# RWKV's small transposes made whole-array ones, token statistics taken from a second, row-wise load of x, and the readers of five broadcasts tied to a weight chunk

## The chip, the cores and the metric

The kernel runs on one core of one Trainium2 chip. The time is the device time of one execution in microseconds, and the time of a kernel is the median of its runs. A core has five engines, each with an instruction stream of its own that runs in program order: TensorE (PE, with its weight loads PEld), VectorE (DVE), ScalarE (ACT), GpSimd (POOL) and SyncE (SP), which here issues the weight transfers.

## The reference, cut to what matters

One block of a model over 256 tokens of width 2048 in float32: a projection of the normed input feeds four branches (an RG-LRU, a forgetting attention "fox", an SSD, an RWKV-7 recurrence), their outputs are gated and merged, and a feed-forward and a gated embedding follow.

```python
xn = rmsnorm(h, mix_norm)                       # mean of squares over 2048 features
proj = xn @ w_in                                # 2048 x 15,000 or so columns
y_a = rg_lru_branch(a_x, a_g, ...)
y_b = forgetting_attention_branch(b_q, b_k, ...)   # q and k normed per head
y_c = mamba2_branch(c_z, c_xbc, c_dt, ...)         # output normed per group
y_d = rwkv7_branch(d_u, ...)
merged = sum(sigmoid(g_j) * (y_j @ w_branch[j]))
h = h + merged @ w_out
h = h + (gelu(conv(hn @ w_up)[gate]) * conv(hn @ w_up)[val]) @ w_down
h = h + sigmoid(rmsnorm(h) @ w_ple_gate) * (p @ w_ple)
```

Inside `rwkv7_branch` the key is normed per head, and the state of each of the eight heads (64 x 64) is advanced token by token; the output is normed per head (mean, variance, `ln_w`, `ln_b`).

## The kernel before, in words

All activations lie feature-major: 128 features on the partitions, 256 tokens along a row. The weights, some 310 MB, are streamed once from HBM in chunks of 512 KB (tile wr, four buffers, line 205, all on SyncE's queue). A matmul in full float32 precision is made of two halves: `split` (lines 208 to 214) has ScalarE round a chunk to its high half wh (the cast, line 212) and VectorE subtract to get the low half wl (line 213), three buffers each. `product` (line 239) then issues a 512-column matmul for wh (the activation's high and low half side by side) and a 256-column one for wl. `gemm_fm` (lines 256 to 302) runs over the chunks of one unit of weights and over its blocks of 128 output features, and keeps the sums in PSUM (tile pg; the branches use pb). So each chunk needs, in this order, its transfer, ScalarE's cast, VectorE's subtraction, and TensorE.

The branches are Python generators (lru, ssd, fox, rwkv). After every block of a product `gemm_fm` calls `hook[0]`, which is `pump` (line 1050): it advances the generator that is first in line by a step, if the credit it keeps allows one. A step's `yield n` says how much credit it costs. `lane` sets one of three priorities (products, branches, TensorE), and a scheduler orders each engine's instructions by these priorities and the dependences, with no knowledge of how long a transfer takes. An engine that reaches an instruction whose input is not there waits, and all that stands behind it on that engine waits with it.

The start: x is loaded feature-major (xT) by `load_x` (line 374) in eight tiles xraw of two feature blocks each. ScalarE squares each tile (line 389), GpSimd sums the squares (line 391), and `token_rstd` (line 401) sums over the partitions with a matmul against ones and takes the reciprocal square root; the result is R (a value per token, on all partitions), and rcol, the same with tokens on partitions. The first unit of weights, w_ax, is multiplied as x arrives; `evac_raw` (line 412) copies its sums out and multiplies by R. `load_after` (line 422) has GpSimd write one column of a tile from another tile, so that the load that ScalarE's queue then issues can't start before that other tile is there. The constants cbr come this way; cbr holds the identity among others.

Five times a branch computes a small row per head, which must then be had on all partitions. GpSimd writes it to DRAM (`bcast_rows`, line 459) and reads it back spread over the partitions (`bcast_full`, `bcast_half`, `head_bcast`, lines 465, 471, 762). The five are ssd_ac (read into tiles d and e; the d tile E is exponentiated on ScalarE, line 693), ssd_rn (line 737), fox_rn (read with the tile gain, line 574), rw_kn (line 831) and rw_gn (line 1009). For rw_gn the source row is finished by a Newton step of two instructions on 8 partitions (`sb<-sb 8x256`), and the first reader on VectorE is `sb<-sb,prm,d`.

The recurrence of RWKV (lines 928 to 986) goes in four blocks of 64 tokens. For each block it loads a tile jc (name e in the profile), transposes three of its parts per head, value and two keys (the last block only the value), with `heads` (line 937): 64 x 64 at a time, the lower head by a matmul with a piece of the identity and the upper one by a transpose (lines 946 to 949), eight per part. A float32 matmul leaves two records in the profile, a transpose one, so a part is 12 records. `kept` (line 953) copies the 128 x 256 result to SBUF.

Of the kernel before, what the change touches and what calls it, by code (L numbers as in the profile page):

```python
# [7 lines left out]
F32 = mybir.dt.float32  # L8
# [3 lines left out]
ALU = mybir.AluOpType  # L12
# [73 lines left out]
def body(tc, T, out, dbg=None):  # L86
# [18 lines left out]
    def add(o, a, b):  # L105
        tt(o, a, b, ALU.add)
# [100 lines left out]

    def split(wr, kn, cols):

        wh = wp.tile([P, kn, cols], F32R, name="wh", tag="wh", bufs=3)  # L210
        wl = wp.tile([P, kn, cols], F32R, name="wl", tag="wl", bufs=3)
        A.copy(wh, wr)  # L212
        V.tensor_tensor(wl, wr, wh.bitcast(F32), op=ALU.subtract)  # L213
        return [(wh[:, i], wl[:, i]) for i in range(kn)]
# [159 lines left out]
    def load_x(k0, kn):  # L374

        if k0 == KD:
            add(xraw[0][:, :S], xraw[0][:, :S], xraw[0][:, S:])
            token_rstd(xraw[0][:, :S], R, rcol)
            return
        xd = xraw[k0 // 2][:, (k0 % 2) * S:(k0 % 2) * S + kn * S]  # L380
        dma_w.dma_start(xd.rearrange("p (k t) -> p k t", k=kn),
                            T["xT"][k0 * P:k0 * P + kn * P].rearrange("(k p) t -> p k t", p=P))
        for k in range(k0, k0 + kn):
            xr = xraw[k // 2][:, (k % 2) * S:(k % 2) * S + S]
            xs.append(split_x(xr, mixc[:, k:k + 1]))
        k = k0 + kn - 1
        if k % 2:
            s = xraw[k // 2]
            act(s, s, AF.Square)
            if k > 1:  # L390
                G.tensor_tensor(xraw[0], xraw[0], s, op=ALU.add)
# [9 lines left out]
    def token_rstd(acc, Rt, col):  # L401
        pt = bank()
        mm2(pt[:, :S], ones_r, acc)
        rstd_of(Rt, pt[:, :S], float(D), EPS, slot(), slot())
        if col is not None:
            pt = bank()
            for t in range(2):
                mm(pt[:, t:t + 1], acc[:, t * P:t * P + P], ones[:, 0:1])
            rstd_of(col, pt[:, :2], float(D), EPS, slot()[:, :2], slot()[:, :2])
    raw = {"ax": []}  # L410

    def evac_raw(lst):
        def f(m, pt):
            s = bslot()
            joined(s, pt)
            mul(s, s, R)
            lst.append(s)
        return f

    gemm_fm(T["w_ax"], xs, evac_raw(raw["ax"]), load_x)  # L420
# [7 lines left out]
    def eslot(shape):  # L428
        return bc_.tile(shape, F32, name="e", tag="e", bufs=3)

# [107 lines left out]
    def fox():  # L538
# [12 lines left out]
        gain = bc_.tile([P, 2], F32, name="gain")  # L551
        ts(gain[:, 0:1], pc("fox_q_gain", 0), 128.0 ** -0.5)
        ts(gain[:, 1:2], pc("fox_k_gain", 0), 1.0)
# [16 lines left out]
        yield  # L570
        qn = []
# [51 lines left out]
    def ssd():  # L623
# [69 lines left out]
        act(E, E, AF.Exp)  # L693
# [40 lines left out]
        yield 6  # L734
        res = []
        for j in range(4):
            stt(yt[j], yt[j], pc("ssd_norm", j), rbc[:, j // 2], ALU.mult, ALU.mult)
# [35 lines left out]
    def rwkv():  # L773
# [26 lines left out]
        yield 6  # L800
        pend = bc_.tile([P, 4, 4], F32, name="pend")
# [6 lines left out]
        for j in range(4):  # L808
# [22 lines left out]
            stt(kk, k_[j], pc("rwkv_kk", j), nbc[j], ALU.mult, ALU.mult)  # L831
# [99 lines left out]
        for c in range(4):  # L931
# [5 lines left out]
            def heads(terms, pt=None):  # L937


                pt = bank() if pt is None else pt  # L940
                for j in range(4):
                    for i, (l, r) in enumerate(terms):
                        for h in (1, 0):
                            hs = H2[h]
                            o = pt[hs, j * 64:j * 64 + 64]
                            if h == 0 and r is ident:
                                transpose(o, l[hs, j], ident[hs, hs])
                                continue
                            mm(o, l[hs, j], r[hs, j] if r is not ident else ident[hs, hs],
                               start=i == 0, stop=i == len(terms) - 1)  # L950
                return pt[:, :S]
# [8 lines left out]
            vc = kept(heads([(jc[:, :, 3], ident)]))  # L960
            yield
            if c < 3:
                btk = kept(heads([(jc[:, :, 1], ident)]))
                yield
                ktk = kept(heads([(jc[:, :, 2], ident)]))
                yield
# [115 lines left out]

    proj("ag", 0, 2)
# [114 lines left out]
    token_rstd(acc1[0], R2, None)  # L1198
# [47 lines left out]
    token_rstd(acc2[0], R3, None)  # L1246
# [31 lines left out]
def layout(inputs):  # L1278
# [11 lines left out]
    for n in ("w_out", "w_up", "w_down", "w_ple_gate"):  # L1290
        r[n] = tiles(f[n][0], S, 4)
    r["xT"] = np.ascontiguousarray(f["x"][0].T)
# [39 lines left out]
```

## Time and profile before

| what | value |
|---|---|
| runs | 1750.37, 1761.89, 1765.18 us (median 1761.89) |
| profiled execution | 1751.44 us |
| its span, first to last instruction | 1749.6 us |
| mean granted clock of TensorE | 0.995 |
| TensorE busy | 1730.1 us (99%), 11621 matmuls |
| VectorE, ScalarE, GpSimd busy | 1237.7 (71%), 942.9 (54%), 102.8 us (6%) |
| HBM read, written | 324.85 MB, 9.48 MB; 191 GB/s over the span |

A row of a timeline gives the start in us from the span's beginning, the time until the last of the xN instructions ended, the engine, the line, the operation, `output<-inputs` by the program's names, the shape, and in brackets how long the engine was idle before it and what ended that. In a row of windows each engine has its busy time and, in parentheses, its number of instructions; the last three columns are the granted clock of TensorE, the busy share of the DMA engines and GB/s.

### The profile page before, as it was taken

Reading aid. Unit: us, or ns where it says so; the run is one execution under the profiler, and the core shown is the slowest. Engines: PE = TensorE matmul, PEld = TensorE weight load, DVE = VectorE, ACT = ScalarE, POOL = GpSimd, SP = SyncE. Lnnn points to the kernel's source line nnn. Section 1 sums busy time; section 2 is a strip of 40 time slices with the busy share of each in tenths; the row PEclk is TensorE's granted clock in tenths of the full one; section 3 lists DMA queues with packets and bytes.
Section 4 is the critical chain, followed back from the end, with each engine's and each line's share of the span. In section 5 each row is a group of like instructions: output and inputs, shape, how many; then the busy total and the mean of one; then the engine's idle time right before and its main releaser. Section 6 shows DMA issues by size and latency. Waiting matters only on the chain.

```text
span 1749.6 us, 29736 instructions
## 1 busy us (share of the span) xinstructions
PE 1730.1 (99%) x11621; PEld 1567.8 (90%) x11621; DVE 1237.7 (71%) x1998; ACT 942.9 (54%) x1422; POOL 102.8 (6%) x160
## 2 busy tenths in 40 slices
PE   8999999999999999999999999999999999999998
PEld 6888888999999989999888888888888888888887
DVE  7788767677789732668678777777777765555666
ACT  6586445556644433545556555555555544444554
POOL 4000000002320100000110000000000000000000
PEclk9999999999999999999999999999999999999999
DMA  7555556556675743565776666656666666656573
GB/s 265 172 178 188 180 174 214 188 183 207 205 214 175 248 137 118 175 198 185 237 227 188 189 190 192 191 186 190 192 189 197 214 208 189 193 190 191 171 227 133
DMA packets 98844, 336.27 MB, mean 192 GB/s; under 512 B 12330, under 2 KB 16592, under 8 KB 98704
## 3 DMA queue, kind: packets, MB, share of 16 engines
q1 hardware_dynamic: 90528, 310.94, 56.3%
q0 software_dynamic: 7456, 21.81, 4.3%
q8 instruction: 91, 1.49, 0.4%
q10 hardware_dynamic: 720, 1.63, 0.3%
q14 instruction: 49, 0.40, 0.1%
HBM read 324.85 MB, written 9.48 MB: 191 GB/s over the span
## 4 chain that ended last, share of the span: by engine, by line
PE 82%; DVE 1%; DMA 0%; issue 0%; ACT 0%; POOLq 0%
PE pg L132 78%; PE pb L135 4%; PE pb L132 1%; DMA e<-fox_rn 0%; DVE wl L213 0%; DVE sb L100 0%; DVE sb L120 0%; DVE s L100 0%; DMA fox_rn<-sb 0%; ACT s L253 0%; POOLq L466 0%
## 5 line engine op out<-in xcount | busy, mean ns | idle before, releaser
L132 PE MATMUL pg<-x,wh 128*128 128x512 f32 (+1 forms) x4384 | 1172.3, 340 | 3.4 <-DVE sb L100 2.7
L213 DVE TENSOR_TENSOR wl<-wr,wh 128x1024 fp32r<-128x1024 f32 (+1 forms) x592 | 716.9, 1212 | 419.6 <-ACT wh L212 412.6
L212 ACT CAST wh<-wr 128x1024 fp32r<-128x1024 f32 (+1 forms) x592 | 615.4, 1041 | 645.7 <-PE pg L132 503.3
L132 PE MATMUL pg<-x,wl 128*128 128x256 f32 (+1 forms) x3344 | 919.7, 283 | 8.8 <-DVE wl L213 8.8
L132 PEld LDWEIGHTS pg<-x,wh 128*128 128x128 f32 x4384 | 748.0, 188 | 89.8 <-issue 4.0
L132 PEld LDWEIGHTS pg<-x,wl 128*128 128x128 f32 (+1 forms) x3344 | 630.4, 189 | 23.7 <-DVE wl L213 11.6
L132 PE MATMUL pg<-f,wh 128*128 128x512 f32 x704 | 243.2, 391 | 0.0
L132 PE MATMUL pg<-f,wl 128*128 128x256 f32 x704 | 195.8, 282 | 0.0
L132 PEld LDWEIGHTS pg<-f,wh 128*128 128x128 f32 x704 | 131.7, 188 | 26.9
L132 PEld LDWEIGHTS pg<-f,wl 128*128 128x128 f32 x704 | 133.2, 189 | 1.0
L132 PE MATMUL pg<-sb,wh 128*128 128x256 f32 x512 | 93.8, 282 | 0.0
L120 DVE SCALAR_TENSOR_TENSOR s<-s,prm 128x255 f32<-128x255 f32 (+1 forms) x176 | 84.0, 477 | 1.7 <-ACT s L127 1.0
L132 PEld LDWEIGHTS pg<-sb,wh 128*128 128x128 f32 x512 | 79.0, 189 | 0.3
L253 ACT COPY s<-pg 128x256 f32<-128x256 f32 x136 | 49.5, 365 | 44.7 <-PE pg L132 44.7
L132 PE MATMUL pg<-sb,wl 128*128 128x256 f32 x256 | 72.6, 285 | 0.0
L100 DVE TENSOR_TENSOR s<-s 128x256 f32<-128x256 f32 (+1 forms) x172 | 70.6, 420 | 1.4
L127 ACT ACTIVATE s<-s 128x256 f32<-128x256 f32 x140 | 56.4, 411 | 17.0 <-DVE s L100 16.7
L100 DVE TENSOR_TENSOR s<-s,pg 128x256 f32<-128x256 f32 x136 | 56.2, 414 | 9.3 <-ACT s L253 8.1
L127 ACT ACTIVATE s<-s,prm 128x256 f32<-128x256 f32 x88 | 52.4, 596 | 0.8 <-DVE s L100 0.8
L127 ACT ACT_TABLE_LOAD x39 | 50.0, 1283 | 1.9 <-PEq L1322 1.2
L132 PEld LDWEIGHTS pg<-sb,wl 128*128 128x128 f32 x256 | 48.3, 189 | 0.3
L132 PE MATMUL pg<-e,wh 128*128 128x512 f32 x128 | 44.9, 391 | 0.0
(232 smaller groups left out, 1189.3 us busy)
## 6 DMA issues: line engine op xcount, KB each, us to landing
wr<-in_w_up_dram SPq DMA_DIRECT2D x176, 512.0 KB, 4.3
wr<-in_w_g_dram SPq DMA_DIRECT2D x128, 512.0 KB, 3.8
wr<-in_w_down_dram SPq DMA_DIRECT2D x88, 512.0 KB, 4.2
wr<-in_w_p_dram SPq DMA_DIRECT2D x76, 512.0 KB, 3.8
wr<-in_w_branch_dram SPq DMA_DIRECT2D x32, 512.0 KB, 3.7
wr<-in_w_out_dram SPq DMA_DIRECT2D x32, 512.0 KB, 3.9
wr<-in_w_ple_gate_dram SPq DMA_DIRECT2D x32, 512.0 KB, 4.7
wr<-in_w_v_dram SPq DMA_DIRECT2D x8, 512.0 KB, 4.2
```

The costliest lines, as they stand in the source:

```text
L100: V.tensor_tensor(o, a, b, op=op)
L120: V.scalar_tensor_tensor(o, a, s, b, op0=op0, op1=op1)
L127: A.activation(o, i, f, **kw)
L132: return f(*a, **kw)
L135: f(*a, **kw)
L212: A.copy(wh, wr)
L213: V.tensor_tensor(wl, wr, wh.bitcast(F32), op=ALU.subtract)
L253: A.copy(o, pt[:, S:])
```

## The change

It has three parts.

First, the statistics of the first norm. The eight squares on ScalarE, the sums on GpSimd and the ones matmuls on TensorE go. Instead x is loaded a second time with tokens on the partitions (xrow, two tiles of 128 x 2048, 1 MB each, on ScalarE's queue, after the last xT tile). `row_stats` squares each with a sum along the row, takes the reciprocal square root on 128 x 2, and spreads it with two small float32 matmuls against the identity to R. It is called at the fifth call of the hook, inside the first unit of w_p; w_ax's sums are copied out unscaled and multiplied by R there.

Second, RWKV's transposes. Of jc each 128 x 128 piece (two parts, both heads) is transposed whole, four to a step: 56 in place of the 80 small operations. ScalarE copies them out in 20 pieces of 64 x 256 in place of 10 of 128 x 256, and the generator has four more steps.

Third, `after_chunk`. It computes a zero on VectorE from the newest wl that the program has made (`stamp`) and puts it into an operand of a broadcast's reader: the bias of E's exponential, gain, and copies of ssd_norm, rwkv_kk and rwkv_ln_w. The scheduler then can't place the reader ahead of that chunk's subtraction.

```diff
+    newest = [None]
     def split(wr, kn, cols):
         A.copy(wh, wr)
         V.tensor_tensor(wl, wr, wh.bitcast(F32), op=ALU.subtract)
+        newest[0] = wl
...
         if k0 == KD:
-            add(xraw[0][:, :S], xraw[0][:, :S], xraw[0][:, S:])
-            token_rstd(xraw[0][:, :S], R, rcol)
             return
...
-        k = k0 + kn - 1
-        if k % 2:
-            s = xraw[k // 2]
-            act(s, s, AF.Square)
-            if k > 1:
-                G.tensor_tensor(xraw[0], xraw[0], s, op=ALU.add)
...
-    gemm_fm(T["w_ax"], xs, evac_raw(raw["ax"]), load_x)
+    gemm_fm(T["w_ax"], xs, evac_raw(raw["ax"], False), load_x)
...
+    xrow = [eslot([P, D]) for _ in range(2)]
+    for t in range(2):
+        load_after(xrow[t], T["xrow"][t * P:t * P + P], xraw[7])
+    stamp = bc_.tile([P, 32], F32, name="stamp")
...
+    def after_chunk(o=None, src=None):
+        z = cells(1)
+        V.tensor_scalar(z, newest[0].rearrange("p k n -> p (k n)")[:, 0:1].bitcast(F32), 0.0, 0.0,
+                        op0=ALU.min, op1=ALU.max)
+        if o is None:
+            return z
+        ts(o, src, 1.0, z, ALU.mult, ALU.add)
+        return o
...
+    def row_stats():
+        z, st = after_chunk(), cells(6)
+        for t in range(2):
+            act(xrow[t], xrow[t], AF.Square, bias=z, accum_out=st[:, t:t + 1])
+        rstd_of(rcol, st[:, 0:2], float(D), EPS, st[:, 2:4], st[:, 4:6])
+        pt, w = bank(), bslot()
+        for t in range(2):
+            tsl = slice(t * P, t * P + P)
+            ts(w[:, tsl], ones, rcol[:, t:t + 1])
+            mm(pt[:, tsl], w[:, tsl], ident)
+        A.copy(R, pt[:, :S])
+        for s in raw["ax"]:
+            mul(s, s, R)
...
-        act(E, E, AF.Exp)
+        act(E, E, AF.Exp, bias=after_chunk())
...
+        gain = bc_.tile([P, 2], F32, name="gain")
+        after_chunk(gain, pcols("fox_q_gain", 2))
...
-            vc = kept(heads([(jc[:, :, 3], ident)]))
-            yield
+            tk = {k: bslot().rearrange(j4, j=4) for k in ((1, 2, 3) if c < 3 else (3,))}
+            for k in (3, 2, 1, 0):
+                if k not in tk and k + 1 not in tk:
+                    continue
+                pt = bank()
+                n = 2 if k + 1 in tk else 1
+                for j in range(4):
+                    transpose(pt[:n * 64, j * P:j * P + P], jc[:, j, k:k + n].rearrange("p a b -> p (a b)"), ident)
+                for h in range(n):
+                    if k + h in tk:
+                        A.copy(tk[k + h][H2[h]],
+                               pt[H2[h]].rearrange("p (j h v) -> p j h v", j=4, h=2)[:, :, h])
+                yield
+            vc = tk[3]
...
         nbc = head_bcast(bcast_rows(w[0][:8], 8, "rw_gn"))
         yield 6
+        lnw = after_chunk(cells(4), pcols("rwkv_ln_w", 4))
         res = []
         for j in range(4):
             y = yc[j]
-            stt(y, y, pc("rwkv_ln_w", j), nbc[j], ALU.mult, ALU.mult)
+            stt(y, y, lnw[:, j:j + 1], nbc[j], ALU.mult, ALU.mult)
...
+    def first_unit():
+        calls[0] += 1
+        if calls[0] == 5:
+            was = cur[0]
+            lane("b")
+            row_stats()
+            lane(was)
+            hook[0] = pump
+    hook[0] = first_unit
     proj("ag", 0, 2)
```

ssd_norm and rwkv_kk are treated as rwkv_ln_w is. What stands on the engines moves at three places. (xN is N instructions of one kind in a row.)

VectorE at rw_gn: the source row's Newton step (`sb<-sb 8x256`), the subtractions of weight chunks (wl) and the readers of the broadcast (with input d). Before:

```order
L124 RECIPROCAL sb<-sb 8x256
L213 TENSOR_TENSOR wl<-wr,wh 128x1024
L100 TENSOR_TENSOR sb<-pg,R 128x256 x3
L100 TENSOR_TENSOR sb<-sb 8x256
L100 TENSOR_TENSOR sb<-pg,R 128x256
L213 TENSOR_TENSOR wl<-wr,wh 128x1024
L120 SCALAR_TENSOR_TENSOR sb<-sb 8x256 x2
L213 TENSOR_TENSOR wl<-wr,wh 128x1024 x3
L120 SCALAR_TENSOR_TENSOR sb<-sb,prm,d 128x256 x2
```

And with the change:

```order
L116 TENSOR_SCALAR stamp<-prm,stamp 128x4
L215 TENSOR_TENSOR wl<-wr,wh 128x1024 x2
L100 TENSOR_TENSOR sb<-sb 128x256 x2
L215 TENSOR_TENSOR wl<-wr,wh 128x1024
L100 TENSOR_TENSOR sb<-sb 128x256 x2
L215 TENSOR_TENSOR wl<-wr,wh 128x1024
L116 TENSOR_SCALAR sb<-pb 8x256
L124 RECIPROCAL sb<-sb 8x256
L215 TENSOR_TENSOR wl<-wr,wh 128x1024
L100 TENSOR_TENSOR sb<-pg,R 128x256 x4
L100 TENSOR_TENSOR sb<-sb 8x256
L120 SCALAR_TENSOR_TENSOR sb<-sb 8x256 x2
```

```order
L120 SCALAR_TENSOR_TENSOR sb<-sb 8x256 x2
L120 SCALAR_TENSOR_TENSOR sb<-sb,stamp,d 128x256 x2
L215 TENSOR_TENSOR wl<-wr,wh 128x1024
L120 SCALAR_TENSOR_TENSOR sb<-sb,prm 128x256 x2
L120 SCALAR_TENSOR_TENSOR sb<-sb,stamp,d 128x256
```

Three subtractions stood between the source and its first readers, now none; the stamp that the readers carry was made five chunks before the source's end, since the generator had been run ahead of it.

TensorE in RWKV's second block (cbr is the identity's tile, e the tile jc, pg the products of weights). Before:

```order
L132 MATMUL pg<-sb,wl 128x256
L132 MATMUL pg<-sb,wh 128x256 x2
L135 MATMUL pb<-cbr,e 64x64 x24
L135 MATMUL pb<-sb,e 64x64 x2
L132 MATMUL pg<-sb,wl 128x256
```

And with the change:

```order
L132 MATMUL pg<-x,wl 128x256
L132 MATMUL pg<-x,wh 128x256 x2
L135 MATMUL pb<-cbr,e 64x128 x4
L135 MATMUL pb<-cbr,e 128x128 x12
L132 MATMUL pg<-x,wl 128x256
```

The 24 small operations, 36 records, have become 16 whole transposes in one run.

ScalarE at the start, from the constants' loads on (its DMA rows are the issues on its queue). With the change:

```order
L416 DMA e<-in_xrow_dram 128x2048 x2
L214 CAST wh<-wr 128x1024
L416 DMA e<-in_lru_bd_dram 128x1024
L416 DMA prm_88<-in_pcol_dram 128x384
L214 CAST wh<-wr 128x1024
```

```order
L256 COPY sb<-pb 128x256 x2
L214 CAST wh<-wr 128x1024 x3
L127 ACTIVATE e,stamp<-e,stamp 128x2048 x2
L214 CAST wh<-wr 128x1024
L127 ACT_TABLE_LOAD
L127 ACTIVATE rcol<-stamp 128x2
```

The rows of x are asked for ahead of two smaller constants. The two squares stand behind 14 casts, all of w_ax's ten and four of w_p's, and one more cast stands between them and the reciprocal root; the eight squares of 128 x 512 that stood among the first casts are gone.

More of the change, by code (lines that the diff above doesn't have):

```diff
@@ L404, in token_rstd, with evac_raw @@
         rstd_of(Rt, pt[:, :S], float(D), EPS, slot(), slot())
[L405 to L409, printed above, removed]
     raw = {"ax": []}
-    def evac_raw(lst):
+    def evac_raw(lst, scaled=True):
         def f(m, pt):
@@ L550, in fox @@
         yield 2
-        gain = bc_.tile([P, 2], F32, name="gain")
-        ts(gain[:, 0:1], pc("fox_q_gain", 0), 128.0 ** -0.5)
-        ts(gain[:, 1:2], pc("fox_k_gain", 0), 1.0)
         fr, frc = bslot(), bslot()
@@ L570, in fox @@
         yield
+        gain = bc_.tile([P, 2], F32, name="gain")
+        after_chunk(gain, pcols("fox_q_gain", 2))
+        ts(gain[:, 0:1], gain[:, 0:1], 128.0 ** -0.5)
         qn = []
@@ L945, in heads @@
                             o = pt[hs, j * 64:j * 64 + 64]
[L946 to L950, printed above, removed]
+                            mm(o, l[hs, j], r[hs, j], start=i == 0, stop=i == len(terms) - 1)
                 return pt[:, :S]
```

28 lines of the change are left out of this document (18 added, 10 removed).

## The prediction

> **What bounds the kernel now.** I read the page first: the busy table and, by line, the chain that ended last.
>
> ```profile
> PE 1730.1 (99%) x11621; PEld 1567.8 (90%) x11621; DVE 1237.7 (71%) x1998; ACT 942.9 (54%) x1422; POOL 102.8 (6%) x160
> PE pg L132 78%; PE pb L135 4%; PE pb L132 1%; DMA e<-fox_rn 0%; DVE wl L213 0%; DVE sb L100 0%; DVE sb L120 0%; DVE s L100 0%; DMA fox_rn<-sb 0%; ACT s L253 0%; POOLq L466 0%
> ```
>
> TensorE is busy for 1730.1 of 1749.6 us, and the chain runs along it for 83%. So time can come or go in three ways only: instructions leave TensorE's own stream, its idle 19.5 us shrink or grow, or its clock is granted more or less often. The view of waits (TensorE's) says what ends its idle time:
>
> ```profile
> PE pg L132 <- DVE wl L213: 8.8, 8, 2.9
> ```
>
> In 8.8 us, eight times, TensorE waits for the low halves of weights (wl, line 213), that is for VectorE to come to them in its own order. What steady work looks like stands in these rows of VectorE's and ScalarE's timelines (start, duration, and in brackets the idle time before and what ended it):
>
> ```profile
> 728.00 1.15 DVE L213 TENSOR_TENSOR wl<-wr,wh 128x1024 fp32r<-128x1024 f32 x1
> 741.45 0.88 DVE L120 SCALAR_TENSOR_TENSOR sb<-sb,prm,d 128x256 f32<-128x256 f32 x2 [0.95 <-DMA d<-rw_gn]
> 738.19 1.05 ACT L212 CAST wh<-wr 128x1024 fp32r<-128x1024 f32 x1 [1.70 <-PE pg L132]
> 740.99 1.06 ACT L212 CAST wh<-wr 128x1024 fp32r<-128x1024 f32 x1 [1.75 <-PE pg L132]
> ```
>
> A wl takes 1.2, a cast 1.05, a three-operand 128x256 on VectorE 0.44; wh has three buffers, so a cast waits for TensorE's end of the chunk three earlier, and two such casts are a chunk apart: 2.8 us.
>
> **The start: row-wise statistics.** The timelines of VectorE, GpSimd and TensorE, and one window of the clock:
>
> ```profile
> 18.69 6.36 DVE L120 SCALAR_TENSOR_TENSOR x<-d,mixc,x 128x256 fp32r<-128x256 f32 x8
> 24.98 4.58 DVE L213 TENSOR_TENSOR wl<-wr,wh 128x1024 fp32r<-128x1024 f32 x3
> 21.45 2.92 POOL L391 TENSOR_TENSOR d<-d 128x512 f32<-128x512 f32 x2 [1.52 <-ACT d L127]
> 26.24 0.39 PE L132 MATMUL pg<-x,wl 128*128 128x256 f32 x1 [2.71 <-DVE wl L213]
> 28.00:32.00 4.00, 4.00 (x16) 3.44 (x16) 2.41 (x4) 1.50 (x4) 2.84 (x3) 0.60 0.95 335
> ```
>
> Eight three-operand steps take 6.36 us, 0.8 each, and the three wl behind them 1.53 each, while GpSimd's additions run; in steady work they take 0.44 and 1.2. TensorE waits 2.71 us for one of them, and the window after it has a granted clock of 0.60 (a window's last three columns are clock, DMA's busy share and GB/s), so 1.6 of its 4 us are lost. The change removes these additions and the squares ahead of them, and both losses hang on them: 2.7 + 1.6 = 4.3, less some 0.3 for the next late thing, the last weight chunks of w_ax: **4.0 gained**, between 1 (only the clock's part, and not all) and 6 (with the small waits of before 18 us).
>
> The Trainium skill, "SBUF — State Buffer", "Who interferes with whom", says that VectorE and GpSimd share a pair of ports under an exclusive lock; the 0.8 against 0.44 apiece agrees. By that rule alone the gain would be the full 4.3.
>
> What it adds, on ScalarE and on the constants' queue:
>
> ```profile
> 19.51 1.29 ACT L127 ACTIVATE x<-d,mixc 128x256 fp32r<-128x256 f32 x3
> 22.17 0.63 ACT L127 ACTIVATE d<-d 128x512 f32<-128x512 f32 x1
> 39.92 1.05 ACT L212 CAST wh<-wr 128x1024 fp32r<-128x1024 f32 x1 [1.60 <-PE pg L132]
> ```
>
> Two squares of 128x2048: 128x256 takes 0.43 and 128x512 0.63, so 0.2 per 256 columns more, 1.8 each, 3.7 for both. They stand behind the cast of the 14th chunk. That is the cast of 39.92, which waits for the end of w_p's first chunk, so w_p began at 39.92 - 2.8 = 37. Four us earlier it begins at 33, TensorE wants the 15th chunk at 33 + 4 x 2.8 = 44.2, and the squares, a cast (1.05) and a wl (1.2) must come before: squares that start by 38 are hidden by w_p's first four chunks. The new 2.1 MB ride on queue 10, as the constants do. The window 32 to 34 shows it share with the weights' queue 1:
>
> ```profile
> DMA packets 246, 0.81 MB, mean 405 GB/s; under 512 B 29, under 2 KB 60, under 8 KB 246
> q10 hardware_dynamic: 133, 0.41, 50.7%
> q1 hardware_dynamic: 113, 0.40, 49.4%
> ```
>
> Half of 405 GB/s carries 0.9 MB of constants and 2.1 MB of x in 15 us, all of it in 7.5; from about 20 that is a landing at 28 to 35. Hidden, with 3 us to spare at worst. The two small fp32 matmuls that spread the result replace the ones and column matmuls of before: nothing.
>
> **rwkv's transposes.** The groups by form, then the stretches in which these run:
>
> ```profile
> L135 PE MATMUL pb<-cbr,e 64*64 64x64 f32 x120 | 18.1, 247 | 0.0
> 617.10:618.80 1.70, 1.69 (x12) 1.16 (x12) 0.00 (x0) 0.00 (x0) 0.00 (x0) 1.00 0.66 241
> 644.67:650.22 5.55, 5.55 (x36) 3.74 (x36) 0.00 (x0) 0.00 (x0) 0.00 (x0) 0.89 0.41 124
> 664.63:669.80 5.17, 5.17 (x36) 3.49 (x36) 0.00 (x0) 0.00 (x0) 0.00 (x0) 0.97 0.83 272
> ```
>
> 120 records, 0.144 apiece in the undisturbed stretches, 17.6 us in all with the disturbed ones. 56 full transposes replace them. Such ones stand elsewhere in the trace, three with one 512-column matmul between them:
>
> ```profile
> 196.50 0.49 PE L135 MATMUL pb<-cbr,sb 128*128 128x128 f32 x3
> 196.74 0.48 PE L132 MATMUL pg<-wl,x 128*128 128x512 f32 x1
> 197.06 0.40 PE L132 MATMUL pg<-wh,x 128*128 128x512 f32 x1
> 348.35 0.38 PE L135 MATMUL pb<-cbr,sb 128*128 128x128 f32 x2
> 348.49 0.36 PE L132 MATMUL pg<-x,wh 128*128 128x256 f32 x1
> 348.69 0.28 PE L132 MATMUL pg<-x,wl 128*128 128x256 f32 x1
> ```
>
> From 348.35 to 348.69 pass 0.34 us, of which one 256-column matmul is 0.117 (a third of 0.35, a 512 and a 256 together): 0.11 per transpose. From 196.50 to 197.06 pass 0.56, less 0.23: 0.11 again. 56 x 0.11 = 6.2, so **11.4 gained**. Bounds: at 0.144 (the nearest record) 8.1, gain 9.5; at 0.19 (the 0.38 of two at 348.35, as if nothing overlapped) 10.6, gain 7.
>
> After the two long stretches the clock falls, and only after those:
>
> ```profile
> 648.00:652.00 4.00, 4.00 (x23) 3.08 (x24) 0.04 (x1) 1.03 (x3) 0.00 (x0) 0.63 0.03 10
> 652.00:656.00 4.00, 4.00 (x40) 3.66 (x39) 1.99 (x3) 0.83 (x2) 0.00 (x0) 0.52 0.25 59
> 668.00:672.00 4.00, 4.00 (x23) 3.40 (x22) 0.00 (x0) 0.74 (x2) 0.00 (x0) 0.69 0.73 272
> 672.00:676.00 4.00, 4.00 (x40) 3.32 (x39) 1.03 (x1) 1.24 (x2) 0.00 (x0) 0.50 0.00 0
> 645.00:688.00 43.00, 43.00 (x473) 37.23 (x474) 12.51 (x19) 11.88 (x21) 1.83 (x3) 0.84 0.38 119
> ```
>
> The four windows lose 4 x (0.37 + 0.48 + 0.31 + 0.50) = 6.6 us; inside the stretches, which end at 650.22 and 669.80, 5.55 x 0.11 + 5.17 x 0.03 = 0.8 of it. About 6.0 fall on the big matmuls behind. After 1.7 us of the same records (617.10) the clock stays at 1.00. The longest new run is 16 transposes, 1.8 us: I take the whole **6.0 as gained** (0 to 6). The ten more copies to SBUF are ScalarE's: ten at 0.36 are 3.6 us, and ScalarE is busy 11.88 of the 43 above; free. Four more steps of the generator move what follows by a chunk.
>
> The Trainium skill, "TensorE: Matmul & The Clock Gate", "Part 4: PE-mode transpose", says that a transpose does not count as work for the clock gate. By that rule the 6.0 would not be gained and rival C would be the case; the rows above cannot tell, since a part of those records are plain matmuls.
>
> **The readers behind a chunk.** ssd_ac, on ScalarE and TensorE:
>
> ```profile
> 159.02 0.63 ACT L127 ACTIVATE d<-d 128x512 f32<-128x512 f32 x1 [3.74 <-DMA d<-ssd_ac]
> 168.72 0.38 PE L132 MATMUL pg<-x,wl 128*128 128x256 f32 x1 [2.85 <-DVE wl L213]
> ```
>
> The exponential holds ScalarE 3.74 us, with casts behind it, and TensorE later idles 2.85. In the new order the exponential stands eleven casts later. Next late are the e tiles of the same broadcast from DRAM, whose readers on VectorE keep their place ahead of a wl. About half remains: **1.3 gained** (0 to 2.85).
>
> ```profile
> 298.24 1.67 DVE L120 SCALAR_TENSOR_TENSOR sb<-sb,gain,e 128x256 f32<-128x256 f32 x4 [4.78 <-DMA e<-fox_rn]
> 301.11 0.39 PE L132 MATMUL pg<-x,wl 128*128 128x256 f32 x1 [1.00 <-DVE wl L213]
> ```
>
> fox_rn holds VectorE 4.78 us, and TensorE 1.00 behind it; one wl now goes ahead of the readers: **1.0 gained** (0 to 1.0). ssd_rn and rw_kn keep their readers' places among the chunks: nothing.
>
> At rw_gn the same rule does the opposite:
>
> ```profile
> 726.33 1.74 DVE L124 RECIPROCAL sb<-sb 8x256 f32<-8x256 f32 x1
> 731.87 0.85 DVE L120 SCALAR_TENSOR_TENSOR sb<-sb 8x256 f32<-8x256 f32 x2
> 734.77 1.23 DVE L213 TENSOR_TENSOR wl<-wr,wh 128x1024 fp32r<-128x1024 f32 x1 [2.05 <-ACT wh L212]
> ```
>
> Before, the source is finished at 731.87 + 0.85 = 732.7 and the first reader starts at 741.45: a trip of 8.7, in which three wl pass. In the new order the stamp was made five chunks earlier and so holds nobody back; the two readers stand right behind the source, and the next wl behind them. RECIPROCAL also stands one chunk later, behind the wl of 728.00: with some 0.4 for the small step that feeds it it ends at 728.00 + 1.15 + 0.4 + 1.74 = 731.3. The same work as before then follows it to the source's end, 732.7 - 729.15 = 3.6: 734.9. Add 8.7 and the readers' 0.88: the wl of 734.77 starts at 744.5 and ends at 745.7. The cast of 740.99 waits for the end of its chunk, so TensorE wants it at 740.99 - 2.8 = 738.2. It idles 745.7 - 738.2 = 7.5, with an idle half clock behind it like that of 28:32 and perhaps 1.5: **9.0 lost** (12.5 with a trip 2 us longer and 3 us of clock, as each rwkv stretch costs above; 1.6 as in rival A).
>
> **Sum.** 4.0 + 11.4 + 6.0 + 1.3 + 1.0 - 9.0 = 14.7. The span falls from 1749.6 to 1734.9, the profiled execution (1751.44) to 1736.7. That execution is 0.6% under the median of 1761.89; the four times known lie in two pairs, 1750 to 1751 and 1762 to 1765. I set the sum against the middle of execution and median, 1756.7: **1742**.
>
> **Rivals.**
> A. The stall at rw_gn is short. If the source ends at 732.7 as before and the trip takes 5 us, since the weights' queue is quiet while TensorE stands, the wl ends at 732.7 + 5 + 0.88 + 1.2 = 739.8: idle 1.6, no loss of clock. For it: nothing in the rows says how fast the trip is on a free queue. Against it: the order puts one more chunk ahead of the source and no wl in the gap. Gain 14.7 + 7.4 = 22: 1735.
> B. The x rows starve the first weight chunks and the start's 4.0 turn into nothing, or the clock's loss stays there. For it: 0.95 busy DMA at 28:32. Against it: w_p's first chunk is wanted only at 33. Gain 10.7: 1746.
> C. The transposes don't do what they are for: 0.19 each, and the clock falls after them as before (0 of the 6.0). Gain 4.0 + 7 + 0 + 2.3 - 9.0 = 4.3: 1752. For it: the clock has fallen only beside this work. Against it: 1.7 us of it leave the clock at 1.00, and the full transposes at 348.35 and 196.50 cost 0.11.
> D. Slower: the x rows land late. The squares stand in ScalarE's order ahead of every later cast, so each us after 38 is an idle us of TensorE. The point from which it decides is 38 + 14.7 = 53. Landing at 65 costs 27 and ends 12 over: 1769. For it: 8 KB rows on one queue beside 512 KB chunks; against it: the equal shares above, by which 53 would need under a quarter of them.
>
> **How the numbers follow.** Forecast 0.50, A 0.17, B 0.13, C 0.12, D 0.08. The forecast's own bounds are about +-10, 1732 to 1752. A stretches the low end to 1726 (start at 6, ssd_ac at 2.85, rest of A's stall gone), C and the early part of D the high end to 1760; outside lie most of D and a tail of A. A measurement can tell about 1%, 17.6 us: under 1744.3 is faster, over 1779.5 slower. The forecast's fall of 14.7 passes that bound in less than half of its cases (0.21 of its 0.50), A mostly (0.15), B and C rarely (0.07: their falls are 4 to 11, and the known times scatter by 0.8%): faster 0.43. D beyond 70 and mishaps of the others: slower 0.07. The rest, 0.50, lies within.
>
> **What would show it.** Right: no TensorE idle over 1 us before 36 and a clock of 1.00 at 28:32; TensorE busy about 11 us less in 64-row work, no half clock behind the rwkv runs; a wait of VectorE for d<-rw_gn of some 8 us and TensorE idle 5 to 9 us just behind it. Wrong: TensorE idle at ScalarE's squares around 44; transposes over 0.15 us apart; no idle time near rw_gn; or the time going to a stage that this text does not name.

## The result and the profile after

The changed kernel takes 1736.53 us (median of 1736.07 to 1736.85) beside 1760.96 for the kernel before: a ratio of 0.987, interval 0.9826 to 0.9914. Measured again on another chip it took 1735.99 beside 1755.20: 0.9896 (0.9872 to 0.9921). One run of all, of the ssd-tied kernel below, took 3813.03 us at a granted clock of 1.0 and is left out. The profiled execution spans 1735.0 us; the sum had said 1734.9. That it is right to 0.1 us is luck: the start and ssd_ac gained 1.7 less than forecast and rw_gn lost 3.0 less, small steps elsewhere made up the rest, and one mechanism in the sum was wrong.

The page and the view of TensorE's waits after the change:

```profile
PE 1716.0 (99%) x11555; PEld 1559.9 (90%) x11555; DVE 1232.9 (71%) x2002; ACT 948.8 (55%) x1428; POOL 92.8 (5%) x155
```

```profile
PE pg L132 <- DVE sb L100: 5.3, 3, 2.9
PE pg L132 <- DVE wl L215: 5.2, 4, 2.5
```

TensorE is busy 14.1 us less. Its waits for wl have fallen from 8.8 to 5.2, but a wait for `sb` has grown from 2.7 to 5.3, with a longest of 2.9 that was not there before.

Both kernels issue the same 4656 low-half matmuls of weights in the same order. The start of the n-th in the trace before, less its start in the trace after, says what has been gained up to there; below this is called the alignment, and a plus means earlier. A half clock is a stretch with a granted clock of 0.5, so that 3.4 us of it lose 1.7. The steps of the alignment by stage:

| stage (us in the trace before) | gained before it | behind it | step | predicted |
|---|---|---|---|---|
| start: w_ax's unit, to 36 | 0 | +5.0 | +5.0 | |
| w_p's first unit, to 49 | +5.0 | +3.3 | -1.7 | start in all: +4.0 |
| ssd_ac, 131 to 253 | +3.0 | +3.3 | +0.3 | +1.3 |
| fox_rn, 293 to 313 | +3.2 | +4.3 | +1.1 | +1.0 |
| rwkv's blocks, 595 to 709 | +4.1 | +21.2 | +17.1 | +17.4 |
| rw_gn, 727 to 736 | +21.4 | +15.4 | -6.0 | -9.0 |
| to the end | +15.4 | +15.0 | -0.4 | 0 |

The start. VectorE's timeline, TensorE's one wait and the clock's window:

```profile
17.96 3.25 DVE L120 SCALAR_TENSOR_TENSOR x<-d,mixc,x 128x256 fp32r<-128x256 f32 x8
21.18 2.36 DVE L215 TENSOR_TENSOR wl<-wr,wh 128x1024 fp32r<-128x1024 f32 x2
14.93 0.39 PE L132 MATMUL pg<-x,wl 128*128 128x256 f32 x1 [2.10 <-DVE wl L215]
28.00:32.00 4.00, 4.00 (x25) 3.52 (x24) 2.94 (x13) 1.22 (x4) 0.00 (x0) 1.00 1.01 412
```

The eight steps take 3.25 in place of 6.36, a wl 1.18 in place of 1.53, the wait of 2.71 is gone and the clock is whole. A wait of 2.10 at 12.8 stands ahead of them. ScalarE has two x steps ahead of a cast there, in both kernels, and they wait for their transfer; first before, then after:

```profile
10.82 0.91 ACT L127 ACTIVATE x<-d,mixc 128x256 fp32r<-128x256 f32 x2 [0.40 <-DMA d<-in_xT_dram]
11.78 0.91 ACT L127 ACTIVATE x<-d,mixc 128x256 fp32r<-128x256 f32 x2 [2.31 <-DMA d<-in_xT_dram]
```

So it is the transfer that came later, not the order. Waits between 11 and 16 us differ by execution: 1.2 to 3.2 in those with the new start, and 1.6 and 1.7 in e1, which has the old one.

What was given back stands in ScalarE's timeline:

```profile
34.97 1.05 ACT L214 CAST wh<-wr 128x1024 fp32r<-128x1024 f32 x1 [1.49 <-DMA wr<-in_w_p_dram]
36.74 1.05 ACT L214 CAST wh<-wr 128x1024 fp32r<-128x1024 f32 x1 [0.71 <-DMA wr<-in_w_p_dram]
37.69 2.00 ACT L127 ACTIVATE e<-e,stamp 128x2048 f32<-128x2048 f32 x1
41.67 1.04 ACT L214 CAST wh<-wr 128x1024 fp32r<-128x1024 f32 x1
```

Casts wait for w_p's chunks, as none did in the trace before, and the squares, some 4 us with the reading of their sums, stand just ahead of the 15th cast.

rwkv's blocks, by form and in one window:

```profile
L135 PE MATMUL pb<-cbr,e 128*128 128x128 f32 x40 | 6.0, 272 | 0.0
L135 PE MATMUL pb<-cbr,e 128*64 128x128 f32 x16 | 2.5, 277 | 0.0
604.00:672.00 68.00, 68.00 (x905) 64.69 (x906) 27.51 (x38) 30.24 (x53) 2.60 (x4) 1.00 0.51 167
```

The clock is 1.00 through all the blocks. The busy times of the groups (6.0 and 2.5) count overlaps with neighbours; the price is measured below.

rw_gn: VectorE, TensorE, ScalarE, then the clock:

```profile
708.29 1.74 DVE L124 RECIPROCAL sb<-sb 8x256 f32<-8x256 f32 x1
709.96 1.15 DVE L215 TENSOR_TENSOR wl<-wr,wh 128x1024 fp32r<-128x1024 f32 x1
711.04 1.39 DVE L100 TENSOR_TENSOR sb<-pg,R 128x256 f32<-128x256 f32 x4
712.80 0.86 DVE L120 SCALAR_TENSOR_TENSOR sb<-sb 8x256 f32<-8x256 f32 x2
719.56 0.88 DVE L120 SCALAR_TENSOR_TENSOR sb<-sb,stamp,d 128x256 f32<-128x256 f32 x2 [5.90 <-DMA d<-rw_gn]
720.36 1.22 DVE L215 TENSOR_TENSOR wl<-wr,wh 128x1024 fp32r<-128x1024 f32 x1
711.49 0.80 PE L132 MATMUL pg<-x,wh 128*128 128x256 f32 x2 [2.87 <-DVE sb L100]
722.86 1.05 ACT L214 CAST wh<-wr 128x1024 fp32r<-128x1024 f32 x1 [1.77 <-PE pg L132]
```

```profile
708.00:712.00 4.00, 1.13 (x8) 0.93 (x7) 3.97 (x6) 3.40 (x4) 0.00 (x0) 0.83 0.42 131
712.00:716.00 4.00, 4.00 (x21) 4.00 (x20) 1.59 (x5) 1.96 (x5) 0.66 (x2) 0.50 0.40 133
716.00:720.00 4.00, 4.00 (x30) 4.00 (x30) 0.44 (x2) 1.05 (x1) 3.43 (x6) 0.82 0.55 143
```

VectorE does wait for the broadcast, with the wl of 720.36 behind it, and TensorE does not mind. It had stood earlier: from 708.62 to 711.49 for the products with R (`sb<-pg,R`), which empty the PSUM of the finished unit. They stand behind RECIPROCAL and a wl, as in the kernel before, but RECIPROCAL now comes one chunk later. Then TensorE ran at half clock, so that it came to the chunk of 720.36 only at 722.9.

### The profile page after: what moved, and what is told of

The parts are those of the page before. It is cut to its first block, busy times and chain, and to the rows that moved or that the text cites. A ratio compares the mean times of both kernels' runs of the same rounds, so it can differ in the third digit from the quotient of the medians.

```text
span 1735.0 us, 29610 instructions
## 1 busy us (share of the span) xinstructions
PE 1716.0 (99%) x11555; PEld 1559.9 (90%) x11555; DVE 1232.9 (71%) x2002; ACT 948.8 (55%) x1428; POOL 92.8 (5%) x155
## 4 chain that ended last, share of the span: by engine, by line
PE 89%; issue 8%; DMA 1%; DVE 1%; ACT 0%; POOL 0%; SPq 0%; DVEq 0%; POOLq 0%
PE pg L132 85%; PE pb L135 3%; PE pb L132 1%; DMA e<-ssd_ac 0%; DMA d<-in_xT_dram 0%; DVE wl L215 0%; DMA wr<-in_w_ax_dram 0%; DVE s L100 0%; DVE e L116 0%; ACT wh L214 0%; DMA ssd_ac<-sb 0%; DVE e L929 0%; DVE e L100 0%; SPq L382 0%; POOL prm L415 0%
## 5 line engine op out<-in xcount | busy, mean ns | idle before, releaser
L127 ACT ACTIVATE s<-s 128x256 f32<-128x256 f32 x140 | 56.6, 412 | 15.4 <-DVE s L100 15.0
L132 PE MATMUL pg<-d,wh 128*128 128x512 f32 x128 | 45.2, 395 | 0.0
```

The costliest lines, as they stand in the source:

```text
L127: A.activation(o, i, f, **kw)
L132: return f(*a, **kw)
```

## The experiments

The medians of before beside these runs lie between 1752.7 and 1760.7, and its single runs spread from 1751 to 1763 on one chip; each ratio is with the runs on the same chip. In these traces TensorE's first product comes up to 1.4 us earlier than in the trace before, whatever the kernel (0.0 in the first trace after, 1.4 in e1), so that much of an alignment belongs to the execution. The transposes in threes, GpSimd's additions and the ssd-tied kernel build on the one called yield 8; the three on the second load build on the ssd-tied one.

**The parts alone.** e1 has the second part of the diff alone, e2 the first, e3 the third.

> The kernel before with the whole-array transposes alone. Theory (each stage pays for itself): TensorE gains in the rwkv stage what it gained with the whole change, 17.2 us (11.2 in the transposes, 6.0 of clock), and VectorE's order at rw_gn stays as before (three weight subtractions between source and readers), so nothing is lost there: span 1749.6 - 17.2 = 1732.4, no half clock at the rwkv blocks. Rival (the denser rwkv work brings the later stall by itself): the 2.9 us of idle and the half clock behind the rwkv blocks appear here too: span about 1738.

1736.52 us, ratio 0.989 (0.9848 to 0.9932), span 1735.7. The rwkv step is +17.1, and there is no loss at rw_gn. But the whole gain is 13.9: 1.3 stood there from the first products on, and at ssd_ac 4.6 us are lost:

```profile
169.42 0.58 PE L132 MATMUL pg<-x,wl 128*128 128x256 f32 x1 [3.77 <-DVE wl L213]
```

```profile
168.00:172.00 4.00, 2.58 (x8) 2.29 (x9) 4.00 (x11) 3.16 (x7) 0.00 (x0) 0.53 0.36 118
172.00:176.00 4.00, 4.00 (x15) 3.34 (x15) 2.92 (x5) 1.01 (x1) 0.00 (x0) 0.61 0.61 172
```

The code there is that of before, where the wait was 2.85 and the clock whole: in this execution the wait is 3.77 and a half clock of 6.8 us follows. The other two kernels without the tie, e2 and e11, have waits of 3.76 and 3.77 there. The theory holds for its stage; the span of one execution does not add up with that of another.

> The kernel before with the row-wise statistics alone. Theory: the start gains what the alignment of the two traces shows behind the first unit of w_p, 3.3 us: span 1746.3, rwkv blocks and their half clock as before. Rival (the second load of x takes the gain back later): within 1 us of before.

1753.46 us, ratio 0.9998 (0.9979 to 1.0017). +4.0 behind w_p's first unit, then the same 3.8 us of idle and half clock at ssd_ac, -4.5. The predicted step came; as a time of its own it is nothing, and the rival's number is right, through a stall that it did not name.

> The kernel before with the five readers tied to a chunk, alone. Theory: fox_rn gains 1.2 and ssd_ac 0.3 us, rw_gn keeps the order of before, so span 1748.1. Rival (the tie at rw_gn is itself what costs): a stall of 3 to 6 us near 730 and a span of 1751 to 1754.

1752.78 us, ratio 0.9989 (0.997 to 1.0008), span 1751.0. No stall near 730, so the tie alone costs nothing at rw_gn. The idle at fox_rn stays at 1.0 and that at ssd_ac at 3.0, with a half clock of 3.4: nothing gained.

**rw_gn's order.** In e1, e2, e3 and e11, which has the first two parts together, VectorE's order at rw_gn is that of before; in the changed kernel it is not. The two other pairs of parts were not run. One waiting step less in the generator puts it back:

```diff
-        yield 9
+        yield 8
```

> The changed kernel with one waiting step less in the rwkv generator (yield 8 in place of 9 ahead of the recurrence), which puts the statistics one chunk earlier and so restores VectorE's order at rw_gn: RECIPROCAL behind the chunk of before, three subtractions between source and readers. Theory (the loss of 5.9 us behind the rwkv blocks comes from that order alone): no idle of 2.9 and no half clock there, span 1735.0 - 5.9 = 1729.1. Rival (the clock falls there for another reason, or the stall moves to the readers): within 1 us of 1735.

1733.24 us, ratio 0.9873 (0.9839 to 0.9907), span 1730.7. VectorE at rw_gn:

```profile
705.35 1.74 DVE L124 RECIPROCAL sb<-sb 8x256 f32<-8x256 f32 x1
707.01 1.15 DVE L215 TENSOR_TENSOR wl<-wr,wh 128x1024 fp32r<-128x1024 f32 x1
708.09 1.06 DVE L100 TENSOR_TENSOR sb<-pg,R 128x256 f32<-128x256 f32 x3
720.39 0.88 DVE L120 SCALAR_TENSOR_TENSOR sb<-sb,stamp,d 128x256 f32<-128x256 f32 x2 [0.88 <-DMA d<-rw_gn]
```

The products come 2.95 us earlier, there is no idle and no half clock, and the +21.0 behind rwkv's blocks stays 21.0 past rw_gn. Two small waits behind it, 0.55 and 0.43, take 1.0 of it, and the fox_rn idle of 1.0 is back in this execution: 4.3 of the 5.9 remain in the span, 3 in the medians. The theory stands for the stage; for the span its price is a quarter too high. The edit moves two things at once, RECIPROCAL and the readers behind the source; e9 below tells them apart.

**The price of a transpose, and the clock.** Each transpose three times:

```diff
                 for j in range(4):
+                    for _ in range(3):
                         transpose(pt[:n * 64, j * P:j * P + P], jc[:, j, k:k + n].rearrange("p a b -> p (a b)"), ident)
```

> The kernel with yield 8, each of the 56 whole transposes issued three times in a row into the same place: 112 more, the longest run 48. Theory (a transpose costs TensorE 0.11 us and counts as work for the clock): span of the yield-8 kernel, 1730.7, plus 112 x 0.11 = 12.3, 1743.0, clock 1.00 in the rwkv blocks. Rival (the skill's rule that transposes do not count as work): runs of 5 us bring the half clock at the two middle blocks, as the 36 small records did before, 6 to 7 us more: about 1749.

Span 1740.7; the rwkv step is 12.5 us less than in the yield-8 kernel, 0.11 for each of the 112. Two runs of 48 last 5.4 us each, from 641.2 and from 656.5:

```profile
640.00:644.00 4.00, 4.00 (x38) 4.00 (x37) 2.43 (x5) 1.42 (x2) 0.00 (x0) 1.00 0.55 162
644.00:664.00 20.00, 20.00 (x268) 19.03 (x268) 3.30 (x4) 7.27 (x16) 1.83 (x3) 1.00 0.43 142
664.00:680.00 16.00, 16.00 (x223) 15.13 (x217) 6.89 (x11) 5.63 (x10) 0.00 (x0) 1.00 0.21 71
```

The clock never falls. As long a run of 64 x 64 operations brought it to a half before, so the length of the run does not do it. The rule of the Trainium skill ("TensorE: Matmul & The Clock Gate", "Part 4: PE-mode transpose") that a transpose does not count as work for the clock gate is not what these whole-array float32 transposes show.

**GpSimd's additions.**

```diff
+    gacc = bc_.tile([P, 2 * S], F32, name="e", tag="e", bufs=3)
...
+        k = k0 + kn - 1
+        if k % 2 and k > 1:
+            G.tensor_tensor(gacc, xraw[0], xraw[k // 2], op=ALU.add)
```

> The kernel with yield 8 and seven additions of 128x512 put back on GpSimd at the start (of the raw x tiles into a spare tile, nobody reads the sum; the squares on ScalarE stay away). Theory (GpSimd's additions slow VectorE's instructions beside them): the x steps take about 0.8 us each in place of 0.41, TensorE waits about 2.7 us near 23, and a half clock may follow: the first product unit ends 2.7 to 4.4 us later than in the yield-8 kernel. Rival (ScalarE's squares in the order of casts were what made VectorE late): x steps stay at 0.41, no wait, within 0.5 us.

VectorE and GpSimd:

```profile
19.48 6.43 DVE L120 SCALAR_TENSOR_TENSOR x<-d,mixc,x 128x256 fp32r<-128x256 f32 x8
22.22 3.02 POOL L391 TENSOR_TENSOR e<-d 128x512 f32<-128x512 f32 x2
```

0.80 a step again, TensorE's waits of 1.1 and 2.8 are back, and the clock is 0.66 in the window 28 to 32. The end of w_ax's unit is 6.4 us later than in the yield-8 kernel, but 1.8 of that stands already at 20 us: 0.7 at the first product, the rest in two earlier waits that grew from 1.5 and 0.3 to 1.9 and 1.1. From 20 to 36 us the alignment rises by 0.4 here and by 5.0 in each of the ten executions that have the new start without the additions. So the additions cost 4.6, near the theory's 4.4, and they cause it, not the squares.

**ssd_ac's other readers.**

```diff
+        z0 = after_chunk()
...
-                    ts(L[:, cs], L[:, cs], col[:, 8 * c + h:8 * c + h + 1], 0.0, ALU.subtract, ALU.min)
+                    ts(L[:, cs], L[:, cs], col[:, 8 * c + h:8 * c + h + 1], z0, ALU.subtract, ALU.min)
```

> The kernel with yield 8, and the readers of the two e tiles of ssd_ac on VectorE tied to a weight chunk too (their second scalar, zero, taken from a stamp). Theory (what is left at ssd_ac is VectorE waiting for e's landing with a weight subtraction behind it): the idle of 2.2 us near 162 goes, span 1730.7 - 2.2 = 1728.5. Rival (ScalarE's order there, with two table loads between casts, sets the wait): idle stays over 1.5.

1728.65 us, the median of three runs, ratio 0.9848 (0.9812 to 0.9885), span 1728.3. The rows of the changed kernel that this mends, and TensorE's waits in this one:

```profile
160.07 1.66 DVE L116 TENSOR_SCALAR e<-e,ssd_col 128x128 f32<-128x128 f32 x8 [1.56 <-DMA e<-ssd_ac]
164.08 1.22 DVE L215 TENSOR_TENSOR wl<-wr,wh 128x1024 fp32r<-128x1024 f32 x1
165.35 0.39 PE L132 MATMUL pg<-x,wl 128*128 128x256 f32 x1 [2.51 <-DVE wl L215]
```

```profile
PE pg L132 <- DVE wl L215: 4.1, 6, 1.6
```

No wait above 1.6 is left, and between 131 and 253 it gains 2.0 us more than the yield-8 kernel does. The exponential that the change tied was one of two things that came late; the e tiles were the next, with some 4 us of VectorE's work ahead of the wl.

**The second load's share.** The x rows in pieces of 2 KB, then an eighth of the load, then an eighth of the squares:

```diff
-        load_after(xrow[t], T["xrow"][t * P:t * P + P], xraw[7])
+        G.tensor_copy(xrow[t][:, 0:1], xraw[7][:, 0:1])
+        nc.scalar.dma_start(xrow[t].rearrange("p (c k) -> p c k", c=4), T["xrow"][t].rearrange("c p k -> p c k"))
...
-    r["xrow"] = f["x"][0]
+    r["xrow"] = np.ascontiguousarray(f["x"][0].reshape(2, P, 4, 512).transpose(0, 2, 1, 3))
```

> The ssd-tied kernel, with the second copy of x stored so that each piece of a row that the load takes is 2 KB in place of 8 KB; all else the same. Theory (queues share the DMA engines by packets, so 8 KB packets take two thirds beside the weights' 3.4 KB ones): the packets of queue 10 rise, w_p's second and third chunks land 1 us or more earlier (32.4 and 34.8 in the ssd-tied kernel), the x rows land later (32.1), and the idle of 0.8 us near 34 goes: 1 us gained at the start. Rival (the bytes alone count, or the packets stay as they are): landings and start within 0.3 us.

1728.02 us, ratio 0.9852 (0.9827 to 0.9878), span 1724.2. Queue 1 carries the weights, queue 10 the x rows. Both from 28 to 30 us, in the ssd-tied kernel and here (packets, MB, share of 16 engines):

```profile
q10 hardware_dynamic: 102, 0.45, 54.5%
q1 hardware_dynamic: 96, 0.39, 47.4%
```

```profile
q1 hardware_dynamic: 146, 0.53, 65.8%
q10 hardware_dynamic: 146, 0.30, 38.4%
```

Nearly equal numbers of packets both times; with smaller packets on the other queue the weights get the larger part. w_p's second and third chunks land at 30.1 and 32.2 (32.4 and 34.8 before), the x rows at 34.8 (32.1), and the idle near 34 is gone. Behind w_p's first unit stands +5.8 in place of +3.4. Of these 2.3 us 0.5 stood there at 14 us, before the x rows were asked for; 1.8 are gained in this stage, where 1 was expected. The medians, on two chips, do not tell the two kernels apart. The Trainium skill, "DMA: Bandwidth & Descriptors", "Queues, rings and completion order", says that an engine goes round its queues packet by packet; these rows agree.

```diff
-        load_after(xrow[t], T["xrow"][t * P:t * P + P], xraw[7])
+        load_after(xrow[t][:, :S], T["xrow"][t * P:t * P + P, :S], xraw[7])
...
-            act(xrow[t], xrow[t], AF.Square, bias=z, accum_out=st[:, t:t + 1])
+            act(xrow[t][:, :S], xrow[t][:, :S], AF.Square, bias=z, accum_out=st[:, t:t + 1])
```

> The ssd-tied kernel with only the first 256 of 2048 columns of the second copy loaded and squared (the statistics leave out the rest). Theory (the x rows' bytes delay w_p's first chunks): no idle near 34 and 44, and the alignment of TensorE's products, which falls from +6 at the end of w_ax's unit to +4 in w_p's first unit, stays at 5 to 6: about 1.7 us gained there. Rival (the fall comes from ScalarE and VectorE work of row_stats): it falls to +4 all the same.

From the end of w_ax's unit to past w_p's first the alignment goes from +4.0 to +4.2, where the ssd-tied kernel goes from +5.7 to +3.4. That alone proves little: this execution came to w_p 1.7 us later, behind a wait of 2.5 and a half clock near 15, and two executions with the whole load and all squares that came as late do not fall either (the changed kernel again, +3.3 to +3.1, and e11, +3.6 to +3.5). The runs with 2 KB pieces and with an eighth of the squares came in at +6.2 and +5.8, so they can tell.

This small edit at the start also moved VectorE's order at rw_gn. VectorE, then TensorE:

```profile
705.01 1.74 DVE L124 RECIPROCAL sb<-sb 8x256 f32<-8x256 f32 x1
707.76 1.39 DVE L100 TENSOR_TENSOR sb<-pg,R 128x256 f32<-128x256 f32 x4
714.66 1.23 DVE L215 TENSOR_TENSOR wl<-wr,wh 128x1024 fp32r<-128x1024 f32 x1 [4.29 <-ACT wh L214]
716.16 0.88 DVE L120 SCALAR_TENSOR_TENSOR sb<-sb,stamp,d 128x256 f32<-128x256 f32 x2 [0.28 <-DMA d<-rw_gn]
708.21 0.51 PE L132 MATMUL pg<-x,wh 128*128 128x256 f32 x2 [2.87 <-DVE sb L100]
```

RECIPROCAL stands one chunk later, as in the changed kernel, but a wl stands ahead of the readers and VectorE hardly waits for the broadcast. The idle of 2.87 is there all the same, with a half clock of 3.4 us. So RECIPROCAL's place brings the stall, without the readers.

> The ssd-tied kernel with the whole second copy loaded, but only its first 256 columns squared (the statistics leave out the rest). Theory (ScalarE's squares are hidden but for the last cast, 0.4 us near 44): the idle near 34 stays, that near 44 goes: 0.4 us gained. Rival (the squares set the fall): 1.7 us gained as with an eighth of the load.

The edit is e9's second pair of lines alone. From +5.8 to +4.7: a fall of 1.1 in place of 2.3. The idle of 0.8 near 34 stays, those of 0.28 and 0.44 near 44 go. In the five executions with the whole load and all squares that came in at +5 or above the fall is 1.8 to 2.3, so the squares add 0.6 to 1.2, more than the 0.4 expected. But they add it only behind late chunks: with 2 KB pieces all squares are there too, start at 35.2 in place of 37.6, and the whole fall is 0.5.

**Without the ties.** The changed kernel less its third part:

> The changed kernel without its third part (the five readers as before), so transposes and row-wise statistics alone; VectorE's order at rw_gn is then that of before. Theory (the ties save the longer stall and the half clock at ssd_ac that the transposes alone and the rows alone showed, 4.6 us, and 1.1 at fox_rn, and cost 5.9 at rw_gn, so they come out near nothing): start +4.0, rwkv +17.2, ssd_ac -4.6, span 1733.0, idle of 3.8 us and a half clock near 163. Rival (the stall at ssd_ac of those two was chance): no half clock there, span 1728 to 1729.

1736.33 us, ratio 0.9878 (0.9839 to 0.9917), span 1733.9. Start +3.5, ssd_ac -3.4 with 3.77 of idle and a half clock of 3.4 us, rwkv +16.9, rw_gn 0. As the theory has it; the median is that of the changed kernel. Between this trace and the first one after, the ties bring 3.7 at ssd_ac and 0.6 at fox_rn, and the changed kernel loses it again at rw_gn. The 0.6 is not a price of the tie, though. VectorE at fox_rn in the changed kernel, in the yield-8 kernel, which has the tie too, and here:

```profile
296.11 1.67 DVE L120 SCALAR_TENSOR_TENSOR sb<-sb,gain,e 128x256 f32<-128x256 f32 x4 [1.30 <-DMA e<-fox_rn]
296.37 1.67 DVE L120 SCALAR_TENSOR_TENSOR sb<-sb,gain,e 128x256 f32<-128x256 f32 x4 [2.61 <-DMA e<-fox_rn]
297.89 1.67 DVE L120 SCALAR_TENSOR_TENSOR sb<-sb,gain,e 128x256 f32<-128x256 f32 x4 [4.22 <-DMA e<-fox_rn]
```

Behind them TensorE idles 0, 1.00, and 0.45 and 0.42. With the tie the idle there is 0 to 1.0, by when the broadcast lands.

**The changed kernel again.**

> The changed kernel itself, beside the others on one chip. Theory: 1735 to 1737 again, some 16 us under the kernel before on this chip, and 3 to 4 over the yield-8 kernel. Rival (the first comparison was helped by slow runs of the kernel before): under 12 below it.

1735.99 us, 19 us under the kernel before on that chip, and 3 over the yield-8 kernel on another. Its profile has the idle of 2.4 us at ssd_ac with a half clock behind it, where the first profile had 2.5 and none. Near 15 us it has a wait of 3.2 and a half clock, where the first had 2.1 and none: the alignment is +3.3 in place of +5.0 at the end of w_ax's unit and still +3.1 behind w_p's first.

## Why the prediction was right or wrong, point by point

**The transposes, 11.4 + 6.0.** Right in both terms: 16.9 to 17.2 in the nine executions of this text with whole transposes and without e5's and e9's changes, 0.11 apiece by e5, no half clock in the blocks. Rival C is out.

**The start, 4.0.** Right in sum, not in its parts. The contention was worth 5.0 in the changed kernel and 4.6 by e6, a little above the 4.3 of its rows. The sign "no TensorE idle over 1 us before 36" failed, by the wait of 2.10 for x, which the change does not cause. The step "hidden, with 3 us to spare" held for the landing (28.5 and 32.3, within 28 to 35) and failed for what else the load delays: the chunks of w_p that it pushes back. The prediction had counted the queue's equal share for x and not what that share takes from the weights. That is rival B's mechanism at about half its price: with pieces of 2 KB 1.8 of the fall of 2.3 is gone. The squares were not hidden either, as 0.6 to 1.2 of the fall goes with them (e10), but only because the late chunks push them back (e8).

**ssd_ac, 1.3.** 0.3 in this pair of traces. The step that failed is "about half remains": VectorE's readers of the e tiles were next late by nearly as much, 2.51 of the 2.85. By e11, without the tie this stage would have lost 3.4, 1.7 of it by the clock; an idle that sometimes brings a half clock is worth more than its own length.

**fox_rn, 1.0.** 1.1 in this pair of traces and 1.2 in the changed kernel again. That the size was hit is partly luck: with the tie in place the idle of 1.00 stays in e3 and in the yield-8 kernel, where the broadcast lands later (e11).

**rw_gn, -9.0.** The loss was right in sign and 6.0 in size, and the mechanism was wrong. "It idles 745.7 - 738.2 = 7.5" took TensorE's own times from the trace before and moved only VectorE's. RECIPROCAL's later place, which the prediction had in its sum only as a delay of the source, stood ahead of the products that empty PSUM, and so stopped TensorE first, for 2.87 us, with 3.1 of lost clock. A TensorE that is six us later needs no wl while the trip lasts. That RECIPROCAL does this without the readers, e9 shows. The trip was also shorter, 5.90 and not 8.7, near rival A's 5. Where TensorE had stood just before (the changed kernel twice, e9) GpSimd waits 1.4 for the row's write and the five transfers land in 2.9 to 3.1 in the median; where it did not (before, e1, e4, e11) these are 2.4 to 2.5 and 4.7 to 4.8. That fits rival A's quiet weights' queue, which no run tested by itself. How much of the stall would be left with the readers behind the source and RECIPROCAL in its old place was not tried. Wrong as well: "four more steps of the generator" as the cause of the shift, since e1 has them and no shift.

**Rival D** did not occur: the rows landed at 32.3, before ScalarE came to them at 37.7.

**The median.** The span was hit to 0.1 us by errors that cancel, and the changed kernel's second profile is 1.6 longer. The time, 1742, is 5.5 high, since it was set against the middle of before's two groups of runs. The changed kernel has no second group. Three of before's first four runs lie in the upper one, so the median falls by 24.4 us where the span falls by 14.7. Before's runs beside the experiments lie at 1751 to 1756 with mean granted clocks of 0.992 to 0.995, and at 1759 to 1763 with 0.987 or 0.988; e2 and e3 have such runs too (1759.94 and 1760.49), while all 31 counted executions of kernels with whole transposes have a clock of 0.995 or more. So the upper group goes away with the small transposes, besides the 17 us in the rwkv blocks. No profile is of that group, so what lengthens it stays open.

## What to carry to other kernels

Sum stage by stage, and in each stage let every engine move: a stall on one engine shifts when the next one needs its data. A sum that comes out to 0.1 us proves nothing about its terms; check each by itself, over several executions. What an added transfer costs is looked for in the transfers beside it, by packets and not by bytes. Where a scheduler sets the order, a waiting step more or less can cost more than the edit brings; read the order of the whole program, and compare stages and not spans where the clock may fall or not.

The version with all three parts, yield 8, both readers of ssd_ac tied and 2 KB pieces beats both kernels: 1728.02 us. Most of that is the transposes and rw_gn's order; the 2 KB pieces show in the alignment and not in the median.

## What the runs showed of the hardware that was not expected

An idle stretch of TensorE of 2.4 to 3.0 us brings a half clock in some executions and none in others: at ssd_ac 2.5 us and none in the changed kernel, 2.4 and 3.4 us of half clock in the same kernel again, 3.0 and 3.4 in e3. At rw_gn 2.9 brought 6.8 in the changed kernel both times and 3.4 in e9. Stretches of 3.8 brought 6.8 in e1 and e2, and 3.4 in e11. The lengths of the half clock are always 3.4 or 6.8 away from the ends, so it seems to be granted in steps of 3.4. The Trainium skill ("TensorE: Matmul & The Clock Gate", "What's actually happening") has a free-running window of 3413 ns, which fits.

Small operations of 64 x 64, 36 records over 5.2 to 6.5 us without any idle, brought 6.8 us of half clock in each of the two blocks, in before, e2 and e3 alike; 48 whole transposes over 5.4 us brought none. Which property of the small operations does it, the quarter of the array or the float32 matmuls among them, was not told apart.
